# Moving 1/rms behind the products in a two-layer hybrid decoder on one core

## The chip, the cores and the metric

The kernel runs on one core of a Trainium2 chip. The core has a matrix engine (TensorE, PE in the profile; its weight loads are listed as PEld), a vector engine (VectorE, DVE), a scalar engine (ScalarE, ACT), a general engine (GpSimd, POOL) and a synchronisation engine (SyncE, SP). SP, ACT and POOL issue the DMAs. Every engine works through its own list of instructions in order and waits for the others by semaphores. The metric is the device time in microseconds of one execution; the median of several runs counts.

## The reference

One inference step of a decoder with two layers on 512 prompt positions and 8 sample rows (520 tokens in all), width 1024, hidden width 2816, all in fp32. A layer is half a feed-forward block, a mixer, and half a feed-forward block again, so there are four feed-forward blocks, called half layers 0 to 3 here:

```python
def _rmsnorm(x, g):
    y = x * lax.rsqrt(jnp.mean(x * x, axis=-1, keepdims=True) + EPS)
    return y * g

def _swiglu(x, wg, wu, wd):
    return (jax.nn.silu(x @ wg) * (x @ wu)) @ wd

for l in range(DEPTH):
    if l == N_A_LAYERS:
        kv = _rmsnorm(x, kv_norm_g) @ w_kv          # shared keys (rotated) and values
    x = x + 0.5 * _swiglu(_rmsnorm(x, norm_g[l, 0]), ffn_w_gate[l, 0], ffn_w_up[l, 0], ffn_w_down[l, 0])
    x = x + mixer(_rmsnorm(x, norm_g[l, 1]))        # l = 0: pooling; l = 1: window attention
    x = x + 0.5 * _swiglu(_rmsnorm(x, norm_g[l, 2]), ffn_w_gate[l, 1], ffn_w_up[l, 1], ffn_w_down[l, 1])
y = _rmsnorm(x, final_norm_g)
```

The factor 1/rms is one number per token. It is the same for all 2816 gate columns and all 2816 up columns of that token.

## The kernel before

**Layout.** x is held turned: eight tiles of 128 model columns by 520 tokens, in SBUF all the time. R is a tile of 128 x 520 that holds 1/rms of every token on all partitions. It is made by `rstd_tok` (line 374: the squares, summed over the eight tiles in `acc`, are reduced over partitions by ten small matmuls, then three Newton steps on VectorE) and `rstd_all` (line 393: spread over partitions by matmuls with ones, then two ScalarE copies). Between the two lie some 13 short VectorE instructions.

**Precision.** Each operand of a matmul is split in a high part (a ScalarE copy to fp32r) and a low part (a VectorE subtraction); `split` (line 240) does it for x and hidden tiles, lines 193 and 194 for weights. A product is then three matmuls (high x high, high x low, low x high) over 260 columns, half of the 520 tokens.

**Half layer** (`ffn`, line 558). The 22 tiles of 128 hidden columns are worked off in parts of 8, 8 and 6 (`PARTS`). After each part the down product adds its share to x: eight output tiles m, for each the matmuls over the part's hidden tiles and one VectorE instruction (line 592). After the last part `after(m)` prepares what the next stage needs from x[m] (for example a split of x times the next norm's g, and its square into `acc`).

A hidden tile is made in one of two ways. `plain_tile` (line 456) makes 96 matmuls: 8 k tiles x 3 terms x gate and up x 2 halves. `strassen_tile` (line 498) takes gate and up and the two halves of the tokens as a 2 x 2 block product in Winograd's form with seven products of 12 matmuls, 84 in all. It needs seven operands on each side. For weights, `Weights.sums` (line 143) makes them: S is loaded a second time by SP, two DMAs on POOL's queue add blocks in place, and VectorE adds two more (lines 163 and 167). For x, the sums `tt` of blocks are made by VectorE once per half layer (lines 547 to 553), two pairs of steps for each of four k. The last product of a Strassen tile is held back (`finish`, line 494) until two products into the next tile, or into the down product.

**How 1/rms comes in before.** The first two tiles (`NU`) of half layers 0, 1 and 3 run on x times g without R ("scaled"); R is multiplied into their gate and up results at lines 482 and 484. Meanwhile `normalised` (line 531) makes x times g times R (line 538), splits it into `xx`, and makes the sums `tt` from it. The next tiles, one more plain one in half layers 0 and 3 and two more in half layer 1, and all Strassen tiles work on `xx` and `tt`. In half layer 2, which follows the key and value projection, all three plain tiles work on `xx`. `NPL` gives the number of plain tiles of each half layer, (3, 4, 3, 3).

**Order.** Weight pieces are got and split five ahead (`W.get`, `W.prefetch`, with six buffers for split pieces and three for raw chunks). `hooks` are small jobs that `plain_tile` runs after every group of 24 matmuls: the reduction, the spreading of R, and steps of `normalised`. The order of the instructions in the file is not the order on the chip: the program is built with a planner (`schedule_with_timeline_sim`, line 1310), which takes, for each engine, the earliest instruction in the file that its own clock says is ready, so that later work can fill a hole. What is marked `later` keeps its order. On the chip the order is then fixed.

**Buffers.** Eight buffers each for the pairs XX (`xh`, `xl`), TT (`th`, `tl`) and HH (`hh`, `hl`). Before, XX holds `xx`, HH the raw x of the first two tiles and then the hidden tiles. PSUM has four buffers of two banks; a plain tile takes two, a Strassen tile two, the reduction one.

## Time and profile before

| | us |
|---|---|
| median of 3 runs (1734.4 to 1736.12) | 1735.6 |
| the profiled execution | 1732.36 |
| its span, first to last instruction | 1730.5 |
| TensorE busy in the span | 1670.3 (97%) |
| VectorE busy | 1196.6 (69%) |
| ScalarE busy | 890.1 (51%) |
| first matmuls of half layers 0, 1, 3 | 16.4, 415.8, 1349.8 |
| keys and values ahead of half layer 2 begin | 784.6 |
| pooling mixer; attention | 385 to 416; 1167 to 1328 |

Times within the profile are microseconds from the first instruction. A group's row gives line, engine, operation, output and inputs by tile names, their shape and the count, then busy time, mean length in ns, and the idle time just before. VectorE's rows give lengths that overlap: the next instruction starts some 0.08 us before the one ahead of it is listed as ended, so what an instruction takes of the engine is the distance between two starts. A window's row gives the stretch and its length, then for each engine busy time and count, then the clock that TensorE was granted and the DMA engines' share. A row of the timeline ends with the idle time before it and who ended it.

### The profile page before, as it was taken

What the parts mean: (1) busy time and instruction counts of PE and PEld (TensorE: products, weight loads), DVE (VectorE), ACT (ScalarE), POOL (GpSimd) and SP (SyncE); (2) the same over time, 40 slices, a digit from 0 to 9 for tenths busy, and PEclk for the clock granted to TensorE, in tenths of its full rate; (3) what the DMA queues carried; (4) which work ended last, traced back from release to release, by engine and by line L of the source; (5) the groups of instructions that cost most, each with busy time, mean ns of one, the idle gap of its engine ahead of it and who ended that gap; (6) DMA issues with size and microseconds to landing.
All of it is one profiled execution on the core that took longest, in us unless ns stands there. A gap on an engine that the chain in (4) does not pass through costs nothing.

```text
span 1730.5 us, 34287 instructions
## 1 busy us (share of the span) xinstructions
PE 1670.3 (97%) x13749; PEld 1653.0 (96%) x13749; DVE 1196.6 (69%) x2331; ACT 890.1 (51%) x1774; POOL 138.7 (8%) x170
## 2 busy tenths in 40 slices
PE   7999999999899999999999999998889999999996
PEld 7899999999899999999999999998789999999996
DVE  6964865877874864868664865868856885684674
ACT  5553643665552652654553643655865563463453
POOL 0101101000101101100101201100000100110100
PEclk9999999999999999999999999999969999999998
DMA  7455745662445745643745845642112555675631
GB/s 197 111 152 134 173 138 135 169 190 70 98 141 129 177 143 133 152 127 82 171 134 135 176 135 137 169 135 71 29 25 74 121 118 142 139 169 138 151 105 50
DMA packets 312606, 223.92 MB, mean 129 GB/s; under 512 B 9072, under 2 KB 288728, under 8 KB 312406
## 3 DMA queue, kind: packets, MB, share of 16 engines
q1 hardware_dynamic: 283760, 173.77, 35.3%
q0 software_dynamic: 22048, 39.72, 14.0%
q10 hardware_dynamic: 6638, 8.23, 1.5%
q8 instruction: 108, 1.77, 0.4%
q14 instruction: 52, 0.43, 0.1%
HBM read 179.84 MB, written 5.04 MB: 107 GB/s over the span
## 4 chain that ended last, share of the span: by engine, by line
PE 88%; DVE 7%; ACT 3%; issue 1%; DMA 1%; ACTq 0%; SPq 0%; POOL 0%; DVEq 0%
PE ps L439 43%; PE ps L414 40%; DVE sm L1011 1%; DVE xl L245 1%; ACT sm L1026 1%; PE ps L1067 1%; DVE tl L245 1%; PE ps L769 1%; PE ps L744 1%; DVE hl L245 1%; DVE wl L194 1%; DVE xb L538 1%; ACT wh L193 1%; DVE xa L538 0%; PE ps L380 0%
## 5 line engine op out<-in xcount | busy, mean ns | idle before, releaser
L193 ACT ACTIVATE wh<-raw 128x512 fp32r<-128x512 f32 (+1 forms) x734 | 447.7, 621 | 585.4 <-PE ps L414 365.5
L194 DVE TENSOR_TENSOR wl<-raw,wh 128x512 fp32r<-128x512 f32 (+1 forms) x734 | 487.7, 676 | 271.9 <-ACT wh L193 259.8
L439 PE MATMUL ps<-th,wh 128*128 128x260 f32 x1200 | 338.8, 283 | 2.0 <-ACT wh L193 1.4
L439 PE MATMUL ps<-tl,wh 128*128 128x260 f32 x1200 | 338.9, 282 | 1.1 <-DVE tl L245 1.0
L439 PE MATMUL ps<-th,wl 128*128 128x260 f32 x1200 | 337.2, 282 | 0.0
L414 PE MATMUL ps<-hl,wh 128*128 128x260 f32 x1600 | 323.7, 283 | 0.0
L414 PE MATMUL ps<-hh,wh 128*128 128x260 f32 x1600 | 322.6, 283 | 0.7 <-ACT R L404 0.7
L414 PE MATMUL ps<-hh,wl 128*128 128x260 f32 x1600 | 322.3, 283 | 0.0
L439 PE MATMUL ps<-xh,wh 128*128 128x260 f32 x900 | 252.1, 282 | 0.5 <-ACT sb L512 0.5
L439 PE MATMUL ps<-xl,wh 128*128 128x260 f32 x900 | 251.9, 282 | 0.0
L439 PE MATMUL ps<-xh,wl 128*128 128x260 f32 x900 | 247.7, 282 | 0.0
L414 PEld LDWEIGHTS ps<-hh,wh 128*128 128x128 f32 x1600 | 246.8, 189 | 0.8 <-ACT R L404 0.8
L414 PEld LDWEIGHTS ps<-hl,wh 128*128 128x128 f32 x1600 | 247.5, 189 | 0.0
L414 PEld LDWEIGHTS ps<-hh,wl 128*128 128x128 f32 x1600 | 247.0, 189 | 0.0
L439 PEld LDWEIGHTS ps<-th,wh 128*128 128x128 f32 x1200 | 225.9, 188 | 2.8 <-ACT wh L193 1.6
L439 PEld LDWEIGHTS ps<-tl,wh 128*128 128x128 f32 x1200 | 225.9, 188 | 1.6 <-DVE tl L245 1.6
L439 PEld LDWEIGHTS ps<-th,wl 128*128 128x128 f32 x1200 | 225.2, 188 | 0.0
L439 PEld LDWEIGHTS ps<-xh,wh 128*128 128x128 f32 x900 | 169.3, 188 | 0.9 <-ACT sb L512 0.9
L439 PEld LDWEIGHTS ps<-xl,wh 128*128 128x128 f32 x900 | 169.4, 188 | 0.0
L439 PEld LDWEIGHTS ps<-xh,wl 128*128 128x128 f32 x900 | 166.7, 188 | 0.0
L158 POOL DMA_DIRECT2D raw<-raw x75 | 64.8, 864 | 1252.6 <-DVE wl L194 480.0
L592 DVE SCALAR_TENSOR_TENSOR x<-ps,x 128x520 f32<-128x520 f32 x96 | 66.9, 698 | 113.4 <-PE ps L414 113.3
(230 smaller groups left out, 2298.4 us busy)
## 6 DMA issues: line engine op xcount, KB each, us to landing
raw<-in_ffn_w_gate_dram SPq DMA_DIRECT2D x87, 512.0 KB, 4.0
raw<-in_ffn_w_up_dram SPq DMA_DIRECT2D x87, 512.0 KB, 5.5
raw<-in_ffn_w_down_dram SPq DMA_DIRECT2D x32, 1024.0 KB, 5.4
raw<-raw POOLq DMA_DIRECT2D x75, 256.0 KB, 3.3
S<-in_ffn_w_up_dram SPq DMA_DIRECT2D x75, 256.0 KB, 5.9
S<-raw POOLq DMA_DIRECT2D x75, 256.0 KB, 4.5
raw<-in_ffn_w_down_dram SPq DMA_DIRECT2D x16, 768.0 KB, 4.3
raw<-in_w_q_dram SPq DMA_DIRECT2D x8, 512.0 KB, 4.1
```

The lines of the kernel that those rows point to most:

```text
L158: G.dma_start(blk(raw, 2, 1), blk(raw, 1, 1), accum_op=ALU.add)
L193: nc.scalar.activation(dh, src, AF.Copy)
L194: nc.vector.tensor_tensor(dl, src, dh.bitcast(F32), op=ALU.subtract)
L245: V.tensor_tensor(lo, src, hi.bitcast(F32), op=ALU.subtract)
L414: T.matmul(banks[:, hf, :H], a[:, kk, :], hcols(b, hf), start=(first and i == 0), stop=(last and i == 2),)
L439: T.matmul(bank[:, :H], a[:, kk, :], b, start=(not more and kk == 0 and i == 0), stop=(kk == 3 and i == 2), skip_group_check=more,)
L538: V.scalar_tensor_tensor(xn, x[kk], gcol(n, kk), R, op0=ALU.mult, op1=ALU.mult)
L592: V.scalar_tensor_tensor(xm, banks[m][:, :, :H], -0.5, xm, op0=ALU.mult, op1=ALU.add)
L744: T.matmul(o, a[:, s], b[:, kk, :], start=(n == 0), stop=(n == 5))
L769: T.matmul(po[:, half * 256 : half * 256 + 256], z[:, tau, c], b, start=(i == 0), stop=(i == len(lst) - 1),)
L1011: V.tensor_tensor_reduce(out=sm[:, e * 256 : (e + 1) * 256], in0=self.pe[e][:, bi * 256 : (bi + 1) * 256], in1=cst[:, mk : mk + 256], op0= ...
L1026: S.activation(part(i), part(i), AF.Exp, bias=nm[:, i : i + 1], accum_out=den[:, i : i + 1])
```

## The change

All gate and up products, plain and Strassen, now run on x times g, without R. R is multiplied in at two places behind them: into the gate's result ahead of the Silu (plain and Strassen tiles alike), and into the result of the down product. The up result keeps no R, since the down product is linear and R is one number per token. `normalised` becomes `sums`, which makes only the sums `tt`, from x times g made by ScalarE; it needs no R and its steps no longer wait for it. Every half layer has two plain tiles, each in the order that was used for scaled tiles; the Strassen tiles work on the same operands as the plain ones (`mov`). The hooks come in another order, with one step of the sums ahead of the reduction. In half layer 2 the operands `mov3` are split during the value projection. The pairs XX and HH change roles, since the operands now live through the whole half layer: in half layers 0, 1 and 3 the operands are in XX and the hidden tiles in HH, in half layer 2 the other way round; attention's tiles move along.

```diff
-NU = 2
-NPL = (3, 4, 3, 3)
-NSTEP = (3, 4, 4, 4, 5)
+NPL = (2, 2, 2, 2)
...
-    def plain_tile(tmp, mov, hs, scaled, hooks, steady=False):
+    def plain_tile(tmp, mov, hs, hooks):
...
-        if scaled:
-            V.tensor_tensor(halves(g), pg[:, :, :H], halves(R), op=ALU.mult)
-            S.activation(t, g, AF.Silu)
-            V.scalar_tensor_tensor(halves(g), pu[:, :, :H], -1.0, halves(R), op0=ALU.mult, op1=ALU.mult)
-            V.tensor_tensor(g, g, t, op=ALU.mult)
-            hidden(g, hs, tmp)
-        else:
-            S.activation(halves(t), pg[:, :, :H], AF.Silu)
-            V.scalar_tensor_tensor(halves(g), pu[:, :, :H], -1.0, halves(t), op0=ALU.mult, op1=ALU.mult)
-            hidden(g, hs)
+        V.tensor_tensor(halves(g), pg[:, :, :H], halves(R), op=ALU.mult)
+        S.activation(t, g, AF.Silu)
+        V.scalar_tensor_tensor(halves(g), pu[:, :, :H], -1.0, halves(t), op0=ALU.mult, op1=ALU.mult)
+        hidden(g, hs)
...
         V.tensor_tensor(halves(g), halves(sa), c[:, :, :H], op=ALU.add)
+        V.tensor_tensor(g, g, R, op=ALU.mult)
         S.activation(t, g, AF.Silu)
...
-    def normalised(tmp, n, ks, xx, tt):
-        for k in ks:
+    def sums(tmp, n, tt):
+        for k in range(4):
             xa = tmp.tile([P, TOK], F32, tag="sa", name="xa")
             xb = tmp.tile([P, TOK], F32, tag="sa", name="xb")
             for kk, xn in ((k, xa), (k + 4, xb)):
-                V.scalar_tensor_tensor(xn, x[kk], gcol(n, kk), R, op0=ALU.mult, op1=ALU.mult)
-                yield
-                xx[kk] = pair(XX, [P, TW])
-                split(tuple(z[:, :TOK] for z in xx[kk]), xn)
-                yield
+                S.activation(xn, x[kk], AF.Copy, scale=gcol(n, kk))
...
-                    xm = halves(x[m])
-                    V.scalar_tensor_tensor(xm, banks[m][:, :, :H], -0.5, xm, op0=ALU.mult, op1=ALU.add)
+                    u = tmp.tile([P, TOK], F32, tag="sb", name="u", bufs=nsb[0])
+                    V.tensor_tensor(halves(u), banks[m][:, :, :H], halves(R), op=ALU.mult)
+                    V.scalar_tensor_tensor(x[m], u, -0.5, x[m], op0=ALU.mult, op1=ALU.add)
...
-        return [lambda: None] * (1 + late) + [rstd_tok, lambda: rstd_all(tmp)] + [lambda i=i: some(i) for i in NSTEP[late:]] + [lambda: some(100)]
+        steps = sums(tmp, n, tt)
+        step = lambda: next(steps, None)
+        return [step, rstd_tok, lambda: rstd_all(tmp)] + [step] * 8
...
-        xx, tt = {}, {}
+        mov3, tt = [], {}
+        steps = sums(tmp, 3, tt)
 
         def during_v(k):
+            mov3.append(pair(HH, [P, TOK]))
+            split(mov3[k], x[k], gcol(3, k))
             if k >= 4:
-                for _ in normalised(tmp, 3, [k - 4], xx, tt):
-                    pass
+                next(steps)
...
-        hooks = [lambda: None, lambda: None, outputs]
-        ffn(2, tmp, None, False, hooks, xx, tt, deferred(4, tmp, "g", XX, mov4))
+        step = lambda: next(steps, None)
+        hooks = [step, outputs] + [step] * 4
+        ffn(2, tmp, mov3, hooks, tt, XX, deferred(4, tmp, "g", HH, mov4))
```

More of the change, by code (lines that the diff above doesn't have):

```diff
@@ L446, in product, with hidden, __init__ @@
                 )
-    def hidden(g, hs, pool=None):
-        if pool is None:
-            hp = pair(HH, [P, TOK])
-        else:
-            hp = tuple(pool.tile([P, TOK], F32R, tag=f"f{t}", name=t, bufs=NU) for t in HH)
+    def hidden(g, hs):
+        hp = pair(hs.tags, [P, TOK])
         split(hp, g)
         hs.append(hp)
-    def plain_tile(tmp, mov, hs, scaled, hooks, steady=False):
+    class Hidden(list):
+        def __init__(self, tags):
+            self.tags = tags
+    def plain_tile(tmp, mov, hs, hooks):
         pg, pu = duo(), duo()
-        if scaled or steady:
-            for k0 in (0, 4):
-                for banks in (pg, pu):
-                    w = W.get()
-                    W.prefetch()
-                    for k in range(k0, k0 + 4):
-                        mm(w, k - k0, mov[k], banks, k == 0, k == KT - 1)
-                    if hooks:
-                        hooks.pop(0)()
-        else:
-            ws = [W.get() for _ in range(4)]
-            for k in range(4):
-                for kk in (k, k + 4):
-                    for i, banks in enumerate((pg, pu)):
-                        mm(ws[2 * (kk // 4) + i], k, mov[kk], banks, kk == 0, kk == KT - 1)
-                if k == 3:
-                    W.prefetch()
+        for k0 in (0, 4):
+            for banks in (pg, pu):
+                w = W.get()
+                W.prefetch()
+                for k in range(k0, k0 + 4):
+                    mm(w, k - k0, mov[k], banks, k == 0, k == KT - 1)
                 if hooks:
@@ L480, in plain_tile @@
         t = tmp.tile([P, TOK], F32, tag="t", name="t")
-        if scaled:
-            V.tensor_tensor(halves(g), pg[:, :, :H], halves(R), op=ALU.mult)
-            S.activation(t, g, AF.Silu)
-            V.scalar_tensor_tensor(halves(g), pu[:, :, :H], -1.0, halves(R), op0=ALU.mult, op1=ALU.mult)
-            V.tensor_tensor(g, g, t, op=ALU.mult)
-            hidden(g, hs, tmp)
-        else:
-            S.activation(halves(t), pg[:, :, :H], AF.Silu)
-            V.scalar_tensor_tensor(halves(g), pu[:, :, :H], -1.0, halves(t), op0=ALU.mult, op1=ALU.mult)
-            hidden(g, hs)
+        V.tensor_tensor(halves(g), pg[:, :, :H], halves(R), op=ALU.mult)
+        S.activation(t, g, AF.Silu)
+        V.scalar_tensor_tensor(halves(g), pu[:, :, :H], -1.0, halves(t), op0=ALU.mult, op1=ALU.mult)
+        hidden(g, hs)
     unfinished = []
@@ L556, in normalised, with ffn @@
             yield
-    def ffn(fi, tmp, first_mov, scaled, hooks, xx, tt, after, before_last=None):
+    def ffn(fi, tmp, mov, hooks, tt, tags, after, before_last=None):
         j = 0
@@ L561, in ffn @@
             last = pi == len(PARTS) - 1
-            hs = []
+            hs = Hidden(tags)
             for _ in range(n):
-                if j == (NU if scaled else NPL[fi]):
+                if j < NPL[fi]:
+                    plain_tile(tmp, mov, hs, hooks)
+                else:
                     while hooks:
                         hooks.pop(0)()
-                if j < NPL[fi]:
-                    raw = scaled and j < NU
-                    plain_tile(tmp, first_mov if raw else [xx[k] for k in range(KT)], hs, raw, hooks, j > NU)
-                else:
-                    strassen_tile(tmp, xx, tt, hs)
+                    strassen_tile(tmp, mov, tt, hs)
                 j += 1
@@ L610, in deferred, with start_hooks @@
         return f
-    def start_hooks(tmp, n, xx, tt, late=0):
-        steps = normalised(tmp, n, range(4), xx, tt)
-        def some(i):
-            for _ in range(i):
-                next(steps, None)
-        return [lambda: None] * (1 + late) + [rstd_tok, lambda: rstd_all(tmp)] + [lambda i=i: some(i) for i in NSTEP[late:]] + [lambda: some(100)]
+    def start_hooks(tmp, n, tt):
+        steps = sums(tmp, n, tt)
+        step = lambda: next(steps, None)
+        return [step, rstd_tok, lambda: rstd_all(tmp)] + [step] * 8
     mov1 = []
@@ L626, in yoco_step @@
         nc.scalar.dma_start(grow[0:48, :], norm_g.rearrange("l n (k p) -> (l n k) p", p=P))
-        xs = [big.tile([NS, 512], F32, tag=t, name="xs") for t in XX]
+        xs = [big.tile([NS, 512], F32, tag=t, name="xs") for t in HH]
         for i in range(2):
@@ L647, in yoco_step @@
         W.load(2)
-        mov0, xx, tt = [], {}, {}
+        mov0, tt = [], {}
         for k in range(KT):
@@ L666, in yoco_step @@
                 S.copy(x[k][:, 0:SP], pk)
-            z = pair(HH, [P, TOK])
+            z = pair(XX, [P, TOK])
             split(z, x[k], gcol(0, k))
@@ L719, in pool_prep @@
                     yield
-        ffn(0, tmp, mov0, True, start_hooks(tmp, 0, xx, tt, 1), xx, tt, deferred(1, tmp, "g", XX, mov1, TW), pool_prep())
+        ffn(0, tmp, mov0, start_hooks(tmp, 0, tt), tt, HH, deferred(1, tmp, "g", XX, mov1, TW), pool_prep())
     with tc.tile_pool(name="pm", bufs=2) as pm:
@@ L784, in band @@
                 )
-                z = pair(HH, [P, TOK])
+                z = pair(XX, [P, TOK])
                 split(z, x[m], gcol(2, m))
@@ L831, in yoco_step @@
             later(nc.sync.dma_start(sink_s[b * 16 : (b + 1) * 16, 0:1], attn_sinks.rearrange("l h -> h l")))
-        xx, tt = {}, {}
-        ffn(1, tmp, mov2, True, start_hooks(tmp, 2, xx, tt), xx, tt, deferred(N_KV, tmp, "g", XX, movk))
+        tt = {}
+        ffn(1, tmp, mov2, start_hooks(tmp, 2, tt), tt, HH, deferred(N_KV, tmp, "g", XX, movk))
     kvs = ExitStack()
@@ L884, in during_k @@
                 rstd_all(tmp)
-        xx, tt = {}, {}
+        mov3, tt = [], {}
+        steps = sums(tmp, 3, tt)
         def during_v(k):
+            mov3.append(pair(HH, [P, TOK]))
+            split(mov3[k], x[k], gcol(3, k))
             if k >= 4:
-                for _ in normalised(tmp, 3, [k - 4], xx, tt):
-                    pass
+                next(steps)
         kb = kv_pass(during_k)
@@ L935, in yoco_step @@
         nc.scalar.dma_start(cst, consts[:, C_MASK : C_MASK + 512])
-        cosq, sinq = pair(HH, [P, TOK], F32)
+        cosq, sinq = pair(XX, [P, TOK], F32)
         nc.scalar.dma_start(cosq, consts[:, C_COS : C_COS + TOK])
@@ L968, in q_evac @@
             rope(qT, banks, cosq, sinq, at, ("rp0", "rp1"))
-            qq = pair(HH, [P, SP])
+            qq = pair(XX, [P, SP])
             split(qq, qT[:, :SP])
@@ L1049, in turn @@
                     n = len(kts) * 256
-                    pp = pair(HH, [P, 512])
+                    pp = pair(XX, [P, 512])
                     split(tuple(z[:, :n] for z in pp), pt[:, :n])
@@ L1167, in o_split @@
             t = len(mov5)
-            z = pair(XX, [P, TW])
+            z = pair(HH, [P, TOK])
             split(tuple(a[:, :SP] for a in z), oT[t])
@@ L1227, in yoco_step @@
                     o_samples(t)
-        after_o = deferred(5, at, "rp0", HH, mov6)
+        after_o = deferred(5, at, "rp0", XX, mov6)
         for m in range(KT):
@@ L1234, in yoco_step @@
     with ff_pool() as tmp:
-        xx, tt = {}, {}
-        yt = {}
+        tt, yt = {}, {}
         def turn(k, xg):
@@ L1264, in final_after @@
             waiting.append((k, xg))
-        ffn(3, tmp, mov6, True, start_hooks(tmp, 5, xx, tt), xx, tt, final_after)
+        ffn(3, tmp, mov6, start_hooks(tmp, 5, tt), tt, HH, final_after)
         turn(*waiting.pop())
```

## The prediction

> **What bounds the kernel now.** I read the page first, then the windows by stage, then the chain of waits and the VectorE timeline at the head of a half layer. The page: TensorE is busy 97% of the span at nearly full clock, VectorE 69%.

> ```profile
> span 1730.5 us, 34287 instructions
> ...
> PE 1670.3 (97%) x13749; PEld 1653.0 (96%) x13749; DVE 1196.6 (69%) x2331; ACT 890.1 (51%) x1774; POOL 138.7 (8%) x170
> ...
> PEclk9999999999999999999999999999969999999998
> ```

> The share is an average over two kinds of stage. These windows (busy time and count of each engine, granted clock) show a stretch of Strassen tiles, the heads of half layers 0 to 3, the last down products of half layer 0, and four short stretches in the head of half layer 0.

> ```profile
> 163.00:235.00 72.00, 72.00 (x603) 72.00 (x602) 57.54 (x98) 44.74 (x87) 8.69 (x10) 1.00 0.66 158
> ...
> 16.00:70.00 54.00, 47.30 (x356) 45.64 (x355) 47.76 (x97) 30.33 (x55) 5.39 (x6) 0.94 0.56 126
> 415.00:477.00 62.00, 57.09 (x464) 55.75 (x464) 53.89 (x116) 32.68 (x57) 6.71 (x9) 1.00 0.40 92
> 784.00:848.00 64.00, 61.08 (x503) 59.89 (x504) 50.23 (x102) 29.06 (x54) 7.44 (x10) 1.00 0.49 117
> 1347.00:1398.00 51.00, 46.83 (x381) 45.53 (x380) 43.14 (x90) 26.39 (x47) 5.27 (x6) 1.00 0.48 109
> ...
> 363.00:387.00 24.00, 24.00 (x204) 24.00 (x203) 22.18 (x46) 17.38 (x41) 0.00 (x0) 1.00 0.53 151
> ...
> 33.25:36.65 3.40, 3.40 (x18) 3.40 (x18) 2.04 (x13) 0.63 (x1) 1.53 (x2) 0.50 0.48 108
> ...
> 50.35:53.65 3.30, 1.40 (x12) 1.25 (x11) 3.30 (x7) 1.28 (x2) 2.26 (x3) 1.00 0.73 122
> 53.75:57.10 3.35, 3.27 (x15) 2.78 (x13) 3.35 (x8) 1.86 (x3) 0.00 (x0) 0.50 0.64 109
> ```

> Between the heads TensorE never stops: 603 matmuls in 72.00 us, 119.4 ns each. At that pace the four heads lose 54.0 - 356 x 0.1194 = 11.5, 6.6, 3.9 and 5.5 us. There the chain of waits runs through VectorE; its timeline shows waits for R and, on TensorE, for a normalised x:

> ```profile
> 40.00 0.75 DVE xa L538
> 40.75 0.67 DVE xb L538
> ...
> 43.91 1.22 DVE xl L245 x2
> ```
> ```profile
> 39.38 0.70 DVE L482 TENSOR_TENSOR g<-ps,R 128x520 f32<-128x520 f32 x1 [2.05 <-ACT R L404]
> ```
> ```profile
> 52.40 0.51 PE L414 MATMUL ps<-xl,wh 128*128 128x260 f32 x2 [1.90 <-DVE xl L245]
> ```

> **The change part by part.** Vector instructions follow one another at these spacings in the timeline: 0.67 us (two tensors and a column), 0.61 (520 columns), 0.60 (weights), 0.34 (260).

> *TensorE.* A plain tile has 96 matmuls, a Strassen tile 84. Plain tiles fall from 3+4+3+3 to 8, so 60 matmuls go: 60 x 0.1194 = 7.2 us, all on the path.

> *Strassen stretches.* Each of 80 tiles gains g = g*R on VectorE (0.61 us) ahead of the Silu. A tile takes 84 x 0.1194 = 10.0 us; VectorE's 14 instructions fill 9 x 0.60 + 2 x 0.61 + 3 x 0.34 = 7.6, then 8.2. Cost 0: the cover is VectorE's spare 1.8 us. The Silu waits 0.6 us longer, and behind it on ScalarE stand the copies of weight pieces (line 193), whose next user on VectorE is line 194; pieces are split five ahead of TensorE, 5 x 12 x 0.1194 = 7.2 us, and ScalarE is busy 44.74 of 72 us, so nobody on the path waits. Five more such tiles also mean five more weight loads into S on SP's queue and ten summing DMAs on POOL's (0.9 to 1.2 us to issue, 4.5 to land). The first Strassen chunk now comes a tile or two earlier; in half layer 1 SP is held until 400.9 by the sinks' DMAs and POOL until 416.3 by output rows, so its sums would land by 422, ahead of 441.9 when it is needed: 0.

> *Down products.* 96 times one instruction becomes two, u = ps*R and x = x - u/2: +0.61 us. The bank is freed as early as before, by u; u takes a buffer of the ring "sb" that the sums and the Strassen tiles use, and no Strassen tile is at work then but the last of its part: 0. In the last part of half layer 0, 7 of them add 4.3 us where VectorE has 24.0 - 22.18 = 1.8 spare: 2.5 us late, less 0.7 that TensorE's reduction matmul (388.1) now waits beyond the last square (387.4): 1.8 us (0 to 3). Half layers 1 and 2 end with TensorE busy behind them: 0 and 0.3 (0 to 0.7). The last one is in the final chain: 0.65. Together 2.8 lost (0.65 to 4.4).

> *Heads.* Per half layer with scaled tiles VectorE loses 8 x 0.67 (L538), 8 x 0.61 (xl) and 2 x 0.61 (one multiply less per plain tile). ScalarE swaps 8 copies for 8 copies. The eight sums steps stay (0.34 + 0.34 + 0.61 = 1.29 us each) but need no R; seven make the first operand set complete: 9.0 us. Against that, one or two plain tiles, 11.5 us of cover each, go. So I count VectorE's work from the start of the head to the seventh step, and compare with when TensorE needs it, 21 matmuls (2.5 us) past the second plain tile.
> Half layer 0: rows 16.66 to 39.38 hold 22.7 us less 5.65 idle = 17.1; then two evacuations of three (3.7), three weight splits (1.8), two weight sums (1.2), 9.0: 32.8, done at 49.5 if the idle time is filled, 55.1 if not; needed at 46.15 + 2.5 = 48.7. Late 0.8 to 6.4; I take the middle, 3.6, since the planner fills idle time only where its own clock sees any.
> Half layer 1: 16.3 (415.6 to 436.04 less 4.1 idle) + 3.7 + 1.2 + 1.2 + sinks 0.6 + 9.0 = 32.0, done at 447.6 to 451.7, needed at 444.4: late 3.2 to 7.3, middle 5.2.
> Half layer 3: 7.5 (1351.8 to 1366.24 less 6.9 idle) + 3.7 + 2.4 + 1.2 + 9.0 = 23.8, done at 1375.6 to 1382.5, needed at 1377.4: late 0 to 5.1, middle 1.7.
> Half layer 2 has no use for R before its first evacuation: x is final at 781. The rows from 784.8 to the last sum at 823.7 hold 36.5 us of work; less 8 x 0.61 (xl; the 8 instructions of line 538 become 8 splits of the same length), with two evacuations (3.7), six weight splits (3.6) and two weight sums (1.2) it is 40.1, done by 827 with the 2.4 us of idle time. TensorE has 404 matmuls from 784.6 (keys, values, two tiles, the reduction), 48.2 us, and comes at 833. Of its 3.9 us 1.0 stays for the first tile's start and the reduction.
> Where a wait for x goes, the next one late is the sum step behind it, hence the balance. Losses before, without what stays (half layer 0: the 2.65 us wait for acc at 30.8 and the half-clock stretch at 33.25, 10 matmuls short, 1.2; half layer 1: 0.9 for R): 7.65, 5.7, 3.9, 5.5.
> The clock: after 50.35:53.65, where TensorE ran 1.40 of 3.30 us, it was granted 0.50 for 3.4 us, 13 matmuls short, 1.5 us. A 3.6 us lateness in half layer 0 brings that again; in half layer 1, where holes up to 1.4 us brought none, I add 0.5 (0 to 1.5). [...]
> Gains: half layer 0, 7.65 - 3.6 - 1.5 = 2.5 (-0.3 to 6.9); 1, 5.7 - 5.2 - 0.5 = 0 (-3.1 to 2.5); 2, 2.9 (1 to 3.9); 3, 5.5 - 1.7 = 3.8 (0.4 to 5.5). Sum 9.2 (-2.0 to 18.8).
> *Moved.* In half layer 0 the reduction over squares is issued one group earlier in the code. TensorE already waits 2.65 us there with 90 matmuls ahead of it, where the code had 72, so the planner places it; at 48 it would cost up to 5 us more. I take 0 and leave 5 to the tail.

> Sum: 7.2 + 9.2 - 2.8 = 13.6 us. The profiled execution took 1732.36 us (span 1730.5), which gives 1718.8; the median of the three runs is 3.2 higher, 1735.6, and gives **1722.0**.

> **Rivals.** (a) *Slower: the added multiply reaches TensorE in the Strassen stretch.* The last product of a tile accumulates into the bank that VectorE reads at L521, and that read now queues behind g*R.

> ```profile
> 191.03 0.42 DVE L521 TENSOR_TENSOR sb<-sb,ps 128x260 f32<-128x260 f32 x1
> ...
> 194.62 0.43 DVE L526 TENSOR_TENSOR g<-ps,t 128x260 f32<-128x260 f32 x1
> ```

> L521 ends at 191.45; the product read at 194.62 takes 12 matmuls, so it began at 193.2: 1.7 us of slack, against 0.61. For it: VectorE is busy 80% there already. If the full 0.61 showed, 80 x 0.61 = 49 us: 1771. It decides from 13.6/80 = 0.17 us a tile. (b) *The heads gain nothing*: the steps still land behind R, heads at their lower bound, 7.2 - 2.0 - 2.8 = 2.4: 1733. For it: VectorE is the chain there, and cover goes as well as work. (c) *All idle time is filled*: 7.2 + 18.8 - 2.8 = 23.2: 1712.4. For it: on TensorE the order already runs products of the first Strassen tile among the third plain tile's matmuls (46.6).

> **How the numbers follow.** 0.2% (3.5 us) is about what a measurement here tells from no change. Forecast (1714 to 1729): 0.62. (a) 0.12. (b) 0.16, a third of it faster, half the same, the rest slower. (c) 0.10, all faster. Faster 0.62 + 0.05 + 0.10 = 0.77; same 0.08; slower 0.03 + 0.12 = 0.15. The bounds of the sum, 7.2 + 18.8 - 0.65 and 7.2 - 2.0 - 4.4, give 1710 and 1735; the range is 1711 to 1736 and leaves out (a) and a few hundredths below.

> **What would show it.** Right: 60 fewer matmuls at lines 414 and 439; no hole in TensorE in the Strassen stretches; VectorE near 82% of them; half layer 1's head losing about what it loses now, the others less; the pool mixer starting a little later. Wrong: TensorE waiting for L521 or for the Silu in every tile; holes of 4 us and a halved clock at each head; a longer wait for the sum of squares.

## The result and the profile after

The changed kernel takes 1744.51 us (median of 6 runs, 1741.13 to 1748.45), the kernel before on the same chip 1734.2 us (6 runs, 1733.57 to 1736.12). The ratio is 1.0059 with a 95% interval from 1.0042 to 1.0076: slower by 10.3 us, where 13.6 us of gain were forecast (1722.0, range 1711 to 1736). The profiled execution took 1745.72 us with a span of 1744.0, which is 13.4 us more than the span of 1730.5 before; of these 3.0 are the two executions' distances from their medians.

The page of the changed kernel:

```profile
span 1744.0 us, 34399 instructions
...
PE 1667.9 (96%) x13689; PEld 1655.0 (95%) x13689; DVE 1275.7 (73%) x2487; ACT 909.5 (52%) x1812; POOL 147.8 (8%) x180
...
PEclk8999999999899999998999999999979999999998
```

The 60 matmuls are gone (13749 to 13689), and TensorE is still busy for about as long, because part of its work ran at half clock (a granted 0.50): the mean granted clock is 0.973 against 0.985 before, and three slices outside attention and the end now show an 8.

The windows of the changed kernel (stretch, length, busy time and count of PE, PEld, DVE, ACT and POOL, granted clock, DMA share, GB/s): a stretch of Strassen tiles, the heads of half layers 0 to 3, the last down products of half layer 0, and two stretches inside heads.

```profile
173.00:245.00 72.00, 72.00 (x605) 72.00 (x604) 61.22 (x106) 44.20 (x85) 8.76 (x10) 1.00 0.67 169
16.00:70.00 54.00, 43.33 (x338) 43.06 (x337) 43.56 (x90) 34.91 (x64) 6.91 (x8) 0.87 0.58 133
418.00:480.00 62.00, 54.47 (x424) 54.00 (x423) 50.00 (x113) 37.31 (x67) 6.48 (x10) 0.89 0.40 92
794.00:858.00 64.00, 56.82 (x451) 56.47 (x450) 42.62 (x89) 30.87 (x58) 9.19 (x12) 0.92 0.49 115
1357.00:1408.00 51.00, 46.30 (x366) 46.02 (x365) 38.68 (x84) 30.93 (x56) 6.10 (x7) 0.93 0.49 114
363.00:387.00 24.00, 24.00 (x203) 24.00 (x202) 24.00 (x51) 16.41 (x41) 0.86 (x1) 1.00 0.45 120
...
30.20:43.75 13.55, 5.79 (x27) 5.83 (x28) 10.62 (x26) 7.66 (x13) 2.64 (x3) 0.50 0.79 169
...
444.50:453.40 8.90, 8.16 (x37) 8.06 (x38) 4.55 (x11) 3.55 (x7) 0.00 (x0) 0.50 0.01 2
```

Between the heads nothing has changed: 605 matmuls in 72.00 us, VectorE at 85%. Each of the four heads has fewer matmuls than its counterpart before, and each has a granted clock under 1. In the last row 37 matmuls run in 8.90 us, 0.24 us each, at a granted clock of 0.50: TensorE is at work, but its products of 260 columns start 0.217 us apart instead of 0.1197.

To put numbers on stages I add up, over neighbouring matmuls, the distance from start to start less what the first of them needs at full clock (0.1197 us for 260 columns, which is 0.46 ns a column; I took the same for other widths, a narrow one counted as 128 columns, an estimate: in the trace of before 256 columns take 0.118 us, 128 columns and fewer 0.11). The sum is what TensorE lost, by waits and by clock together:

| lost on TensorE, us | half layer 0, head | pooling mixer | half layer 1, head | half layer 2, head | attention | half layer 3, head | end | sum |
|---|---|---|---|---|---|---|---|---|
| before | 19.0 | 5.6 | 7.8 | 5.8 | 42.2 | 7.0 | 5.9 | 93.3 |
| changed | 20.5 | 8.8 | 12.6 | 12.3 | 41.7 | 8.6 | 9.3 | 113.9 |

20.6 us more are lost, and 60 x 0.1194 = 7.2 us of matmuls are saved: 13.4, the difference of the spans. The heads lose 14.4 us more, the pooling mixer and the end 6.6, attention 0.5 less.

**What the heads wait for.** TensorE's timeline in half layer 1 and at the reduction of half layer 0 (start, length, the row's instructions; in brackets the idle time before them):

```profile
437.31 0.40 PE L412 MATMUL ps<-xh,wl 128*128 128x260 f32 x2
444.49 2.04 PE L398 MATMUL ps<-dg,ones 128*128 128x128 f32 x8 [6.78 <-ACT th L242]
...
37.95 2.26 PE L378 MATMUL ps<-ones,acc 128*128 128x1 f32 x10 [9.93 <-DVE acc L367]
```

Line 398 spreads R over the partitions. It stands in TensorE's list ahead of the next products, and none of them ran in those 7 us. It waits 6.78 us for `dg` (7.06 from start to start); the releaser named, ScalarE's `th`, is not what it waits for, it only ended last. The cause shows on VectorE, where the twelve short instructions of `rstd_tok` (lines 382 to 389) run from 431.89 to 443.59:

```profile
431.89 0.17 DVE L382 TENSOR_SCALAR nv<-ps 128x5 f32<-128x5 f32 x1
431.97 0.42 DVE L533 SCALAR_TENSOR_TENSOR t<-t,xb 128x260 f32<-128x260 f32 x1
432.31 0.69 DVE L192 TENSOR_TENSOR wl<-S,wh 128x512 fp32r<-128x512 f32 x1
432.91 0.17 DVE L383 TENSOR_SCALAR ny<-nv 128x5 int32<-128x5 int32 x1
432.98 0.70 DVE L243 TENSOR_TENSOR tl<-t,th 128x520 fp32r<-128x520 f32 x1
433.59 0.43 DVE L527 TENSOR_TENSOR t<-xa 128x260 f32<-128x260 f32 x1
433.93 0.17 DVE L384 TENSOR_SCALAR ny<-ny 128x5 int32<-128x5 int32 x1
...
442.91 0.43 DVE L532 TENSOR_TENSOR t<-xb,xa 128x260 f32<-128x260 f32 x1
443.25 0.43 DVE L528 SCALAR_TENSOR_TENSOR t<-t,xb 128x260 f32<-128x260 f32 x1
443.59 0.17 DVE L389 SCALAR_TENSOR_TENSOR r_tok<-nt,ny 128x5 f32<-128x5 f32 x1
...
444.06 0.87 DVE L397 TENSOR_SCALAR dg<-ident,r_tok 128x128 f32<-128x128 f32 x4
```

Each of them needs the one ahead of it. Between every two the planner has put one or more others: steps of the sums (lines 527 to 533 and 243), which no longer need R, weight pieces (192) and the copies of the sinks. Before, when the steps needed R, the same chain went from 428.51 to 430.71 with nothing between its links:

```profile
428.51 0.16 DVE L384 TENSOR_SCALAR nv<-ps 128x5 f32<-128x5 f32 x1
428.70 0.17 DVE L385 TENSOR_SCALAR ny<-nv 128x5 int32<-128x5 int32 x1
...
430.71 0.17 DVE L391 SCALAR_TENSOR_TENSOR r_tok<-nt,ny 128x5 f32<-128x5 f32 x1
```

So it takes 11.7 us from first start to last start instead of 2.2, and TensorE stands still meanwhile. The same happens in half layers 2 and 3 (6.7 and 4.2 us from start to start).

In half layer 0 it is ScalarE that makes `acc` late; its timeline in the changed kernel:

```profile
28.11 0.63 ACT L191 ACTIVATE wh<-raw 128x512 fp32r<-128x512 f32 x1
33.34 0.63 ACT L191 ACTIVATE wh<-S 128x512 fp32r<-128x512 f32 x1 [4.60 <-DMA S<-raw]
33.88 0.62 ACT L363 ACTIVATE sq<-x 128x520 f32<-128x520 f32 x1
```

The first Strassen tile now comes a tile earlier, so the copy of its piece S comes earlier in ScalarE's list, ahead of the last two squares. It waits 4.60 us for a DMA, and the squares wait behind it: the last one starts at 35.03. Before, ScalarE's last square and the reduction that needs it stood at

```profile
28.54 0.62 ACT L365 ACTIVATE sq<-x 128x520 f32<-128x520 f32 x1
...
30.81 1.25 PE L380 MATMUL ps<-ones,acc 128*128 128x1 f32 x10 [2.65 <-DVE acc L369]
```

**What the end waits for.** VectorE at the last down product of half layer 3:

```profile
1693.56 0.70 DVE L571 TENSOR_TENSOR u<-ps,R 128x520 f32<-128x520 f32 x1 [1.45 <-PE ps L412]
1694.18 0.55 DVE L192 TENSOR_TENSOR wl<-raw,wh 128x384 fp32r<-128x384 f32 x1
1694.64 0.69 DVE L571 TENSOR_TENSOR u<-ps,R 128x520 f32<-128x520 f32 x1
1695.25 0.69 DVE L572 SCALAR_TENSOR_TENSOR x<-u,x 128x520 f32<-128x520 f32 x1
```

Before, x was written in one step, by the instruction that stands where u's stands now:

```profile
1683.65 0.70 DVE L592 SCALAR_TENSOR_TENSOR x<-ps,x 128x520 f32<-128x520 f32 x1 [1.45 <-PE ps L414]
```

Now x does not come one instruction later (0.61 us) but three (1.69 us): a weight piece and the second tile's u, both ready by the time that u was written, stand between. TensorE's wait for the transposes grows from 1.89 to 3.57 us between starts.

### The profile page after: what moved, and what is told of

It reads as the page before. It is cut to its first block, busy times and chain, and to the rows that moved or that the text cites. A ratio compares the mean times of both kernels' runs of the same rounds, so it can differ in the third digit from the quotient of the medians.

```text
span 1744.0 us, 34399 instructions
## 1 busy us (share of the span) xinstructions
PE 1667.9 (96%) x13689; PEld 1655.0 (95%) x13689; DVE 1275.7 (73%) x2487; ACT 909.5 (52%) x1812; POOL 147.8 (8%) x180
## 4 chain that ended last, share of the span: by engine, by line
PE 88%; DVE 6%; ACT 3%; DMA 2%; issue 1%; SPq 0%; ACTq 0%; DVEq 0%
PE ps L437 46%; PE ps L412 37%; DVE sm L990 1%; DVE wl L192 1%; PE ps L720 1%; PE ps L1046 1%; ACT sm L1005 1%; DMA pr<-in_bands_dram 1%; PE ps L745 1%; PE ps L378 0%; ACT wh L191 0%; PE ps L398 0%; DVE xl L243 0%; DMA S<-in_ffn_w_up_dram 0%; DVE tl L243 0%
## 5 line engine op out<-in xcount | busy, mean ns | idle before, releaser
L412 PE MATMUL ps<-hh,wh 128*128 128x260 f32 x1376 | 281.5, 285 | 3.6 <-DVE mx L990 2.2
L412 PE MATMUL ps<-hl,wh 128*128 128x260 f32 x1376 | 281.0, 283 | 0.0
L412 PE MATMUL ps<-hh,wl 128*128 128x260 f32 x1376 | 279.2, 283 | 0.0
L412 PEld LDWEIGHTS ps<-hh,wh 128*128 128x128 f32 x1376 | 212.8, 189 | 5.0 <-DVE mx L990 2.9
L437 PE MATMUL ps<-xl,wh 128*128 128x260 f32 x720 | 201.6, 283 | 0.0
L437 PE MATMUL ps<-xh,wh 128*128 128x260 f32 x720 | 201.5, 282 | 0.0
L437 PE MATMUL ps<-xh,wl 128*128 128x260 f32 x720 | 197.5, 282 | 0.0
L571 DVE TENSOR_TENSOR u<-ps,R 128x520 f32<-128x520 f32 x96 | 67.1, 700 | 107.0 <-PE ps L412 107.0
L437 PEld LDWEIGHTS ps<-xl,wh 128*128 128x128 f32 x720 | 135.5, 188 | 0.0
L437 PEld LDWEIGHTS ps<-xh,wh 128*128 128x128 f32 x720 | 135.4, 188 | 0.0
```

The costliest lines, as they stand in the source:

```text
L412: T.matmul(banks[:, hf, :H], a[:, kk, :], hcols(b, hf), start=(first and i == 0), stop=(last and i == 2),)
L437: T.matmul(bank[:, :H], a[:, kk, :], b, start=(not more and kk == 0 and i == 0), stop=(kk == 3 and i == 2), skip_group_check=more,)
L571: V.tensor_tensor(halves(u), banks[m][:, :, :H], halves(R), op=ALU.mult)
```

## The experiments

The theory after the result: the order is to blame. Work that lost its dependence on R was put between the instructions that make R ("interleaved chain"), and a copy that waits for a DMA was put ahead of the squares. Rivals: two plain tiles are too little cover whatever the order ("too little cover"); the added multiplies cost it ("added work"). A planner's order can be held with `issue_after(ins)`: what is written under it goes into its engine's list behind `ins`, with no further wait.

All kernels, in the table of lost time as above:

| kernel | median, us | ratio to before (95%) | hl 0 | pool | hl 1 | hl 2 | att. | hl 3 | end |
|---|---|---|---|---|---|---|---|---|---|
| e1 R chain first | 1743.03 | 1.0048 (1.0033 to 1.0063) | 21.4 | 10.4 | 7.4 | 8.8 | 47.4 | 4.3 | 11.0 |
| e2 before, both multiplies | 1744.9 | 1.0059 (1.0044 to 1.0074) | 20.3 | 10.9 | 9.7 | 6.9 | 42.7 | 7.1 | 9.6 |
| e3 changed, plain tiles (3, 4, 3, 3) | 1757.63 | 1.0132 (1.0117 to 1.0147) | 17.5 | 10.7 | 11.2 | 11.9 | 50.4 | 7.1 | 9.9 |
| e4 e1 and S behind | 1738.43 | 1.0026 (1.0014 to 1.0039) | 15.6 | 10.2 | 7.4 | 9.6 | 50.1 | 4.4 | 11.0 |
| e5 before, g*R alone | 1735.17 | 1.0002 (0.9993 to 1.0011) | 20.1 | 5.7 | 7.8 | 5.7 | 43.9 | 7.1 | 6.0 |
| e6 changed, no u in the last part | 1735.8 | 1.0001 (0.9989 to 1.0013) | 22.3 | 5.4 | 12.6 | 6.2 | 41.1 | 8.5 | 5.8 |
| e7 e4, sums of half layer 2 later | 1738.94 | 1.0020 (1.0011 to 1.0030) | 16.1 | 9.0 | 7.4 | 8.6 | 47.9 | 4.4 | 9.3 |
| e8 combination | 1717.01 | 0.9898 (0.9881 to 0.9914) | 10.7 | 5.9 | 2.4 | 9.5 | 44.6 | 0.9 | 5.8 |
| e9 e8, S of half layer 2 held | 1716.26 | 0.9895 (0.9877 to 0.9912) | 11.3 | 5.5 | 2.4 | 3.9 | 51.6 | 0.9 | 5.8 |
| e10 e9, two plain tiles | 1718.45 | 0.9906 (0.9890 to 0.9921) | 16.8 | 5.5 | 9.0 | 2.7 | 42.3 | 4.4 | 5.8 |
| e11 e9, R in hidden from part 2 | 1715.04 | 0.9892 (0.9876 to 0.9907) | 10.4 | 5.8 | 2.4 | 3.5 | 49.0 | 0.9 | 5.8 |
| e12 e4 again | 1740.53 (one run) | | 15.7 | 10.4 | 7.4 | 9.3 | 49.0 | 5.8 | 11.0 |

The kernel before, which ran beside them, had medians of 1734.34 (e1 to e4), 1734.95 (e5 to e8) and 1733.85 us (e9 to e12).

### e1: the R chain first

```diff
-        V.tensor_scalar(dg2, ident[:, 112:120], r_tok[:, 4:5], None, op0=ALU.mult)
+        r_last[0] = V.tensor_scalar(dg2, ident[:, 112:120], r_tok[:, 4:5], None, op0=ALU.mult).ins
...
+            with tc.issue_after(r_last[0]):        # in sums(), around both steps
                 V.tensor_tensor(t1, b11, b12, op=ALU.subtract)
...
-        return [step, rstd_tok, lambda: rstd_all(tmp)] + [step] * 8
+        return [lambda: None, rstd_tok, lambda: rstd_all(tmp)] + [step] * 8
...
-            split(mov3[k], x[k], gcol(3, k))
+            with tc.issue_after(r_last[0]):
+                split(mov3[k], x[k], gcol(3, k))
```

> The changed kernel with one difference of order: on VectorE every instruction of the eight sums steps, and in half layer 2 also the low parts of mov3, is queued behind the last dg of rstd_all, so that the short instructions of the R chain follow one another. The first hook is empty instead of a step. Same work, same number of instructions. Theory 'interleaved chain' (the sums steps sit between the short dependent instructions of the R chain, R comes 4 to 10 us late, TensorE stands still and its clock is halved afterwards): the holes ahead of the spreading of R in half layers 1, 2 and 3 (7.1, 6.7, 4.2 us) shrink below 1.5 us each and their half-clock stretches (13.65, 10.2, 6.8 us) go; the hole of 10.2 us in half layer 0 loses some 3 to 5 us, since the copy of S still stands ahead of the squares on ScalarE; the sums come later and cost up to 5 us in half layer 1. 1717 to 1732 us. Rival 'too little cover' (two plain tiles are too short whatever the order): the same time is lost at the first Strassen product that needs the sums, 1738 to 1750. Rival 'added work' (the multiplies by R in Strassen tiles and down products cost it): order does not matter, 1740 to 1750.

Measured: 1743.03 us, within the rivals' ranges and not the theory's. The places say otherwise. VectorE's timeline in half layer 1:

```profile
434.77 0.17 DVE L383 TENSOR_SCALAR nv<-ps 128x5 f32<-128x5 f32 x1 [1.57 <-PE ps L379]
...
437.45 0.17 DVE L390 SCALAR_TENSOR_TENSOR r_tok<-nt,ny 128x5 f32<-128x5 f32 x1
...
438.78 0.87 DVE L398 TENSOR_SCALAR dg<-ident,r_tok 128x128 f32<-128x128 f32 x4
```

The chain takes 2.7 us from first to last start again, the waits for `dg` in half layers 1, 2 and 3 are gone, and these three heads lose 13.0 us less than in the changed kernel (12.6 + 12.3 + 8.6 against 7.4 + 8.8 + 4.3). In half layers 1 and 3 that is less than the kernel before loses (7.8 and 7.0). The gain was given back elsewhere: attention lost 47.4 us instead of 41.7, the pooling mixer and the end 3.3 us more, half layer 0 another 0.9. Half layer 2 has a new wait of 4.6 us, ahead of its first plain tile, which e7 and e9 take up; the hole at the reduction of half layer 0 shrank by 2.0 us where 3 to 5 were expected. So the interleaving is shown where it was said to be, and the kernel's time needed other causes too. (The empty first hook and the held steps were not tried apart.)

### e2 and e5: the added multiplies on the kernel before

```diff
         V.tensor_tensor(halves(g), halves(sa), c[:, :, :H], op=ALU.add)
+        V.tensor_tensor(g, g, R, op=ALU.mult)                                # e2 and e5
...
-                    V.scalar_tensor_tensor(xm, banks[m][:, :, :H], -0.5, xm, op0=ALU.mult, op1=ALU.add)
+                    V.tensor_tensor(halves(u), banks[m][:, :, :H], halves(R), op=ALU.mult)   # e2 alone
+                    V.scalar_tensor_tensor(x[m], u, -0.5, x[m], op0=ALU.mult, op1=ALU.add)
```

> The kernel before with only the added VectorE work of the change: g = g*R in each Strassen tile, and u = ps*R with x = x - u/2 in the down products. Its x already carries R, so R is counted twice here and the result is not the reference's; the instructions and their lengths are those of the change. Rival 'added work': most of the 10 us show here, 1743 us or more, and each Strassen tile loses time. Theory 'interleaved chain': nothing in the Strassen stretches, and only the ends of half layers 0 and 3 lose (pool mixer 1 to 3 us, the two transposes of the last down product 1 to 3, the last subtraction 0.6): 1736 to 1742. My record's own terms, 2.8 for the down products and 0 for the Strassen tiles, give 1737.

> The kernel before with g = g*R added in the Strassen tiles and nothing else; R is counted twice in the gate, so the result is not the reference's. It splits the 10.6 us that the added multiplies cost together. If the subtraction behind the down products (u, then x) is what costs, this kernel keeps the lost TensorE time of the kernel before in every head, ahead of the pooling mixer (5.6 us) and at the end (5.9 us), and takes 1731 to 1740 us, the width being attention, whose order the planner finds anew (41.7 to 50.4 us lost so far). If the multiply in the 80 Strassen tiles costs, 1742 us or more, with losses in the stretches of Strassen tiles.

Measured: 1744.9 us, in the range of "added work" and above the theory's, and 1735.17 us. The 75 multiplies of the Strassen tiles here cost nothing (ratio 1.0002). The two-step update makes the difference, 9.7 us: against e5 the pooling mixer loses 5.2 us more, the end 3.6, half layer 1 1.9, half layer 2 1.2. TensorE's wait for the squares at the pooling mixer:

```profile
389.38 0.28 PE L746 MATMUL ps<-th,xl 128*128 128x256 f32 x1
392.63 0.56 PE L380 MATMUL ps<-ones,acc 128*128 128x1 f32 x2 [2.97 <-DVE acc L369]
```

Before, TensorE had no hole over 0.25 us at this reduction and one of 1.05 behind it; now there are 3.25 us from start to start. "Added work" is half right: not in the 75 tiles, where VectorE has room, but in the two-step updates; e6 undoes those of the four last parts alone, which stand in a chain.

### e3: the old numbers of plain tiles

```diff
-NPL = (2, 2, 2, 2)
+NPL = (3, 4, 3, 3)
```

> The changed kernel with the old numbers of plain tiles, (3, 4, 3, 3) instead of (2, 2, 2, 2): 60 more matmuls, 7.2 us at the pace of 0.1194 us. Rival 'too little cover': the longer cover removes the holes, 1725 to 1738. Theory 'interleaved chain': the holes ahead of the spreading of R stay as they are, since R is needed by the first plain tile's evacuation however many follow; 1748 to 1755, a little less if the later first chunk of Strassen weights frees ScalarE's squares in half layer 0.

Measured: 1757.63 us, 13.1 more than the changed kernel, for 7.2 us of matmuls, and above both ranges. The heads of half layers 0 to 3 lose 3.0, 1.4, 0.4 and 1.5 us less, less together than the matmuls cost, and attention 8.7 more, without which the time would lie in the theory's range. The holes ahead of line 398 in half layers 1 and 2 stay (6.4 and 6.7 us), the one in half layer 3 shrinks from 4.2 to 2.4. While R is late, more cover gains less than it costs.

### e4 and e12: S behind R in half layer 0

```diff
+        W.behind = [r_last[0], S.copy(R[:, SP:], pr2).ins]
...
+                if self.behind and 8 <= self.ns < 16:      # pieces of the first Strassen chunk
+                    for ins in self.behind:
+                        order.enter_context(self.tc.issue_after(ins))
```

> As the kernel with the R chain first, and in half layer 0 the weight pieces of the first Strassen chunk (S among them, whose DMA lands at 33 us) are copied on ScalarE behind R's copies and subtracted on VectorE behind the last dg. Theory 'interleaved chain', second part (the copy of S, queued ahead of the last squares, makes acc late): the wait for acc falls from what the kernel with the R chain first still has to 2 to 3 us, as in the kernel before, and R follows; 4 to 8 us better than that kernel, 1711 to 1726. If the squares were late for another reason, no difference.

Measured: 1738.43 us, 4.6 better than e1, near the low end of the gain expected. TensorE's distance ahead of the reduction fell from 8.17 to 1.37 us, the head from 21.4 to 15.6. The range expected for the whole kernel was missed, as in e1, mainly because of attention, which lost 50.1 us, 8.4 more than in the changed kernel; the pooling mixer and the end lost another 3.1 more. Whether attention's loss is scatter or order, e12 asked with the same kernel:

> The kernel with S behind, profiled once more with nothing changed: its attention lost 50.1 us of TensorE time where the changed kernel lost 41.7, with another order of the same instructions. If that is the order, it loses 49 to 51 again; if it is scatter from one execution to the next, anything from 41 to 51.

It lost 49.0 us in attention, and 5.8 instead of 4.4 in the head behind it. That alone fits both readings, since 49.0 lies in 41 to 51 as well. The traces of the other kernels decide it. e4, e7 and e12 run attention's instructions in one and the same order on TensorE, VectorE and ScalarE, and lose 50.1, 47.9 and 49.0 us; e9 and e11 share another order, and lose 51.6 and 49.0. So one order scatters by up to 2.6 us in these five profiles. e6, e8 and e10, whose lists on TensorE and ScalarE are closer to the changed kernel's than to e4's, lose 41.1 to 44.6; e1 and e3, closer to e4's, lose 47.4 and 50.4. Most of the loss belongs to the order: when something ahead of attention moves, the planner can list the same instructions differently.

### e6: R in the hidden tiles of the last part

```diff
         S.activation(t, g, AF.Silu)
+        if hs.last:
+            V.tensor_tensor(t, t, R, op=ALU.mult)
...
+                    if last:
+                        V.scalar_tensor_tensor(xm, banks[m][:, :, :H], -0.5, xm, op0=ALU.mult, op1=ALU.add)
+                    else:
```

> The changed kernel with one part undone: in the last part of each half layer R goes into t behind the Silu (one more multiply on VectorE in each of the six tiles), and x is again updated by one instruction from the bank. If the two-step update is what delays the reduction ahead of the pooling mixer and the transposes at the end, the losses there go back from 8.8 and 9.3 us to 5.6 and 5.9, the heads stay: 1738 us (1734 to 1742). If the second multiply per tile reaches TensorE in the last part, 1744 or more.

Measured: 1735.8 us, 8.7 less than the changed kernel and the same as before (ratio 1.0001). VectorE at the end, to be read against the four lines above:

```profile
1685.08 0.70 DVE L575 SCALAR_TENSOR_TENSOR x<-ps,x 128x520 f32<-128x520 f32 x1 [1.45 <-PE ps L412]
1685.69 0.55 DVE L192 TENSOR_TENSOR wl<-raw,wh 128x384 fp32r<-128x384 f32 x1
1686.16 0.69 DVE L575 SCALAR_TENSOR_TENSOR x<-ps,x 128x520 f32<-128x520 f32 x1
```

The pooling mixer (8.8 to 5.4) and the end (9.3 to 5.8) go back to what they lost before. Half layer 2 was not expected: its head falls from 12.3 to 6.2, because x's last tile leaves half layer 1 earlier. In the changed kernel u of that tile started at 784.44 and x at 788.27, with five other instructions between; here x starts at 781.72, R's chain 5.1 us sooner (1.7 of them gained ahead of half layer 1), the chain, still interleaved, takes 9.8 instead of 11.1 us, and the distance ahead of line 398 is 2.3 instead of 6.7 us. The wait of 7.06 us in half layer 1 stays to the hundredth, as does the 4.2 in half layer 3.

### e7: the sums of half layer 2 behind the low parts of mov3

```diff
-            if k >= 4:
-                next(steps)
+            if k == KT - 1:
+                ahead[0] = low.ins                # sums are queued behind this one
...
-        hooks = [step, outputs] + [step] * 4
+        hooks = [two, outputs] + [two] * 3
```

> The kernel with R first and S behind, and in half layer 2 the sums queued behind the last low part of mov3, two steps a hook, instead of being spread through the value projection. There TensorE stood 6.3 us ahead of the first plain tile, waiting for a low part of mov3. If the sums steps between the low parts made that wait, the loss of that head falls from 9.6 us to 4 to 6 and nothing new appears at its first Strassen tile: 1734 us (1729 to 1740, the width again being attention). If the hole has another cause (the copies of R, the rotation of the keys on VectorE), 1737 to 1741 and the hole stays.

Measured: 1738.94 us, no gain, and the wait ahead of the first plain tile is still 4.7 us. The cause I had named was wrong, and the time lies where another cause would put it. ScalarE's timeline points at a cause that was not on the list:

```profile
809.90 0.72 ACT L530 ACTIVATE xb<-x,gT 128x520 f32<-128x520 f32 x1
815.45 0.63 ACT L196 ACTIVATE wh<-S 128x512 fp32r<-128x512 f32 x1 [4.82 <-DMA S<-raw]
815.98 0.57 ACT L908 COPY vtok<-ps 128x512 f32<-128x512 f32 x1
```

Again a copy of S waits for its DMA, ahead of the copy that empties a bank of transposed values; TensorE's next plain product, at 816.60, waits for that copy. e9 puts this to the test.

### e8 to e11: everything together, and what is then left

e8 is e7 with e6's update and `NPL = (3, 3, 2, 3)`. e9 holds the first chunk's Strassen pieces behind other instructions, in half layers 0 and 2:

```diff
+        if first:                                  # first plain tile, half layers 0 and 2
+            W.behind = [a.ins, b.ins]              # its multiply by R, its Silu
```

e10 is e9 with two plain tiles everywhere, e11 is e9 with e6's update from the second part on.

> The kernel with the order of half layer 2, plus R in the hidden tiles of the last part, plus one more plain tile in half layers 0, 1 and 3 (36 more matmuls, 4.3 us). If the causes are the order at the heads, the two-step update at the ends and the sums that land some 3 us late at the first Strassen tile: 4 us less than before at the pooling mixer, 5 at the end, about 4 us in each of the three heads against 4.3 us of matmuls: 1724 us (1716 to 1732), faster than both kernels. If the sums are not what the first Strassen tiles wait for, the plain tiles only cost: 1730 or more.

> The combination, with the Strassen pieces of the first chunk in half layers 0 and 2 queued behind the first plain tile's Silu on ScalarE and behind its multiply by R on VectorE. In the combination ScalarE stood 6.1 us for the DMA of S (copy at 806.0 us), ahead of the copies that empty the banks of the transposed values, and TensorE waited 5.9 us for a bank. If that copy is the cause, the head of half layer 2 falls from 9.5 us lost to 2 to 4 and nothing else moves but attention: 1710 us (1705 to 1716). If the banks wait for something else, 1714 to 1720.

> The same with (2, 2, 2, 2) plain tiles: 36 matmuls (4.3 us) less. If with R early the sums are the next thing late at two plain tiles, as the waits of 1.4 to 2.1 us for th and tl at the first Strassen products of half layers 0, 1 and 3 say, these heads lose some 4, 5 and 3.5 us more (half-clock stretches included), and the kernel is 6 to 10 us slower than the one with (3, 3, 2, 3). If cover is no matter, it is 4 us faster than that one.

> The kernel with S held, and R in the hidden tiles of the second part too, so that only the first part's down products keep the two-step update. VectorE trades eight u for eight t*R in each half layer. The ends are already free of u, the middle down products were costed at nothing: within 0.2% of that kernel. If the second multiply per tile reaches TensorE in a full part of eight Strassen tiles, slower by up to 20 us (0.6 us in 32 tiles).

Measured: 1717.01 us for e8, near the good end of its range. Against e7 the head of half layer 0 loses 5.4 us less, half layer 1 5.0, half layer 3 3.5, pooling mixer and end 6.6, against 4.3 us of matmuls. e9 does in half layer 2 what was expected (9.5 to 3.9 us; the wait of 5.9 us is 0.95), and its time, 1716.26, is the same as e8's and misses its range (1705 to 1716) by a little, since attention's order came out 7.0 us worse. e10 answers the question of cover: with R early, two plain tiles lose 5.5, 6.6 and 3.5 us more in the heads of half layers 0, 1 and 3 than e9. TensorE's first wait at the Strassen tiles of half layer 1 is

```profile
443.08 0.39 PE L445 MATMUL ps<-th,wh 128*128 128x260 f32 x1 [1.44 <-ACT th L247]
```

for the sums. In time e10 is only 2.2 us behind e9, not 6 to 10, as it saves 4.3 us of matmuls, loses 1.2 less in half layer 2, and drew an attention that loses 9.3 less. e11, 1715.04 us, is within the 0.2% of e9 that was expected and has the lowest median of all, 1.1% below the kernel before; its page:

```profile
span 1712.6 us, 34360 instructions
...
PE 1660.7 (97%) x13725; PEld 1647.8 (96%) x13725; DVE 1255.3 (73%) x2455; ACT 897.9 (52%) x1794; POOL 142.5 (8%) x174
...
PEclk9999999999999999999999999998979999999998
```

The 8 in the first slice of the changed kernel is gone, as are those at half layers 1 and 2.

## Why the prediction was wrong, step by step

| step | predicted gain, us (bounds) | measured |
|---|---|---|
| TensorE, 60 matmuls fewer | 7.2 | 7.2 |
| Strassen stretches | 0 | 0 |
| head of half layer 0 | 2.5 (-0.3 to 6.9) | -1.5 |
| head of half layer 1 | 0 (-3.1 to 2.5) | -4.8 |
| head of half layer 2 | 2.9 (1 to 3.9) | -6.5 |
| head of half layer 3 | 3.8 (0.4 to 5.5) | -1.6 |
| down products: pooling mixer | -1.8 (-3 to 0) | -3.2 |
| down products: attention | -0.3 (-0.7 to 0) | 0.5 |
| down products: end | -0.65 | -3.4 |
| sum | 13.6 | -13.3 |

**TensorE and Strassen stretches: right.** The count is exact. g*R costs nothing on its 75 tiles in e5, and rival (a) is out: in the changed kernel's stretch TensorE has no hole, and VectorE, forecast at 82%, is at 85%.

**Heads: the step that failed.** It counted VectorE's work up to the seventh sums step and took idle time in which steps can run as free. That idle time lay between instructions that wait for one another. On an engine that works through a list, an instruction put there does not only use the gap, it delays whatever comes behind by what it is longer than the gap: instructions 0.20 us apart got one or more neighbours, most of 0.34 to 0.61 us, at eleven places. The step asked when the sums would be late; what was late was R, which they now ran in front of on the same engine. "Half layer 2 has no use for R before its first evacuation" missed the same thing: the matmuls of line 398 stand in TensorE's list during the projection of keys and values, and TensorE waited 6.7 us there. The lateness of the sums, 3.6, 5.2 and 1.7 us, is nearer to another kernel: in e10, where R is kept first, the holes over 0.6 us at the first Strassen products add up to 2.9, 3.2 and 2.6 us from start to start, not all of them for the sums. So the sentence that named the next thing late ("the next one late is the sum step behind it") named the wrong thing.

**Moved: wrong.** The reduction in half layer 0 was taken as placed by the planner at no cost, with up to 5 us left to the tail. The wait for the sum of squares grew from 2.9 to 10.2 us, not because the reduction was moved but because the first Strassen chunk was, past the squares on ScalarE's list. That the chunk comes earlier was noted, and was followed on SP's and POOL's queues and in half layer 1 alone, not on ScalarE's in half layer 0, where e4 gets 5.8 us of the head back.

**The clock: mis-sized.** 2.0 us were taken for all heads. In the changed kernel the stretches at half clock in the heads and the pooling mixer last 13.65, 3.41, 13.65, 10.24 and 6.83 us. From the end of each hole to the end of its stretch TensorE ran at that clock for 5.86 + 3.41 + 8.92 + 7.46 + 6.57 = 32.2 us. Its 136 matmuls there start 0.217 us apart at 260 columns and 0.213 at other widths; at full clock it is 0.1197 at 260, 0.118 at 256 and 0.11 below. That makes 13.4 us lost, against 2.8 by the 29 matmuls of the two stretches of 3.41 us before, so some 10.6 of the 20.6 us are clock. That is an account, not an experiment: no run holds the clock.

**Down products: mis-sized by a factor of three.** 2.8 us were predicted, 9.7 measured (e2 against e5) and 8.7 (the changed kernel against e6). The term counted u's own 0.61 us; the planner put other ready work between u and x as well, so x came 1.69 us later at the end. "Half layers 1 and 2 end with TensorE busy behind them: 0" looked only at TensorE. The late x also makes R late in half layer 2: in e6 that head loses 6.1 us less, a part of it because the chain there was also listed 1.3 us tighter.

**The rivals.** (b), heads that gain nothing, was nearest, but it had the steps landing behind R where they were listed in front of it, and its bound for the heads was still too good: no row of before shows R's chain with foreign work in it, and none of my bounds asked what it would cost. The list of what would show the forecast wrong had two of the three signs seen, holes of 4 us with a halved clock at each head and a longer wait for the squares.

**What stays open.** How much of attention's 41.1 to 51.6 us is avoidable was not tried; nor was an order written out by hand there. In half layer 2 the shares of the late x and of the tighter chain in e6's gain were not tried apart.

## What to carry to other kernels

When a change takes a dependence away, ask not only what becomes free to run earlier but what it will run in front of: work that is ready early is put between the links of a chain that is not, and on an engine that works through its list in order each link then pays for its neighbour (2.2 us became 11.7 here). Price an instruction added to a chain by what can be listed between it and the next link, not by its own length. And where a planner fixes the order, judge a change by the stage it touches as well as by the total: an untouched attention moved by up to 10 us here, as much as the whole effect.

## What was not expected of the hardware

**What a hole costs beyond itself.** The wait of 7.06 us in half layer 1 was followed by 8.9 us at a granted clock of 0.50; at the spacings of full clock its 37 matmuls need 4.3 us and a wait of 0.9 (1.1 from start to start) lies in it, so some 3.7 us more went. The step of the grid that began at 446.58 was broken by the wait for R's copies (the first product starts at 447.50), and the clock came back only behind the next one, at 453.40. The other steps at half clock bear it out: over the same part of the two traces all eight with 2.38 us of matmuls or less (0.217 us for 260 columns) were followed by another, and all six with 2.60 or more by full clock.
